# One fused block for the first two feed-forward tiles, and attention operands laid over other memory

## The chip, the cores and the metric

The kernel runs on 1 core of one Trainium2 chip. The metric is the device time of one execution in microseconds (us). Before the change it is 1364.41 us, the median of 3 runs (1362.14 to 1365.34). About the engines' names: PE is TensorE (matmuls; PEld is its weight load), DVE is VectorE, ACT is ScalarE, POOL is GpSimd, and SP is SyncE, which here only issues transfers (DMAs), in order, from its queue (SPq).

## The reference

One layer of a streaming encoder is computed for two sets of tokens with the same weights: 1024 frames of a new stream (the prompt) and 32 frames of a running one (the sample), 1056 tokens in all, model width 1024.

```python
h = x * (1 + sc1) + sh1                       # sh, sc, g: modulation, silu(c) @ w_ada + b_ada
mq, mk, mv, mo, mi, mf, fq, fk, fv, ff, gu, gv = split(h @ w_in)
hm = mlstm(mq, mk, mv, mi, mf)                # 4 heads, matrix memory
hf = fox(fq, fk, fv, ff)                      # 8 heads, softmax attention with a forget term
hg = gu * (ws @ layer_norm(gv) + bs)          # spatial gate
x = layer_norm(ALPHA * x + (1 + g1) * (concat(hm, hf, hg) @ w_o))
h = x * (1 + sc2) + sh2
y = (silu(h @ w_gate) * (h @ w_up)) @ w_down  # width 2816 = 22 tiles of 128
x = layer_norm(ALPHA * x + (1 + g2) * y)
```

The outputs are both sets' x and the caches of the three mixers.

## The kernel before, in words

**Numbers.** All products are float32 with each operand split in two float32r parts, hi and lo; `gemm` (L110) does three matmuls per 128 rows of depth: hi x hi (L116), hi x lo (L117), lo x hi (L118). A weight unit of 1024 columns is loaded as `raw`, cast to `whi` on ACT (L104) and split to `wlo` on DVE (L105), all in `weights` (L92). There are three buffers of each (`RAW = 3`, `WB = 3`).

**Tokens.** They are cut in two parts: part 0 has tokens 0 to 511, part 1 the other 544. Part 0 is worked on in two halves, 0 to 255 and 256 to 511 (`MM[0]`), or whole (`WIDE`). Part 0's attention queries are done in the first third of the kernel, and part 0 then goes through the output projection, the first normalization and the feed-forward product while part 1's attention heads (`mixers`, L1326) are worked on between its matmuls.

**The stage of the change**, in the order in which `run` (L1341) emits it:

- `wo_range` (L1041): output projection of part 0, first half, then second half. The second half is woven with `ln1` (L1079), the normalization of the first half: the two generators take turns. `ln1` makes the operand of the feed-forward product, `hh` and `hl` (shown as tm_ah and tm_al in the profile).
- `ln1` of the second half, then `fm_unit` for heads 5 to 7 (part 1's queries and keys, fm_g in the profile), whose results `evac_qk` (L358) stores to memory through the tiles qkh, qkl and qkr, and `ln1_res` (L1098) on POOL.
- Pools p1 and sm, both on the right side of the on-chip memory, are closed, and pool mx1, on the same side, is opened over them. It holds the attention's operands (k1, k2, qp, q2, v), softmax tiles and the mLSTM's tiles. A tile in it waits for the tiles that lay at its place.
- `mixers`: for each of the 8 heads `fox` (L737) loads the operands with nine transfers on SP, then for query tiles 4 to 7 does scores (L779, L780), maximum (L783), exponential (L788), division (L796), then transposes (L815), splits (L820, L821) and the product with v (L823, L828). Before head 1 stands `fox_sample` (L861), and heads 1 to 5 are woven with one mLSTM step each (L584).
- The feed-forward loop over groups of tiles: `up` (L1126) for each tile j (gate product, up product, then silu by exponential, logarithm and exponential on ACT, L1143 to L1145, two multiplications on DVE, L1146 and L1147, and the split, L1148 and L1149), then `down` (L1272) for the group. Group 0 takes tiles 0 to 3 before its `down`. After each of tiles 0 to 3 stands `ada` (L170), a modulation unit (20 to 23), which loads its weights into two of the three `raw` buffers and takes one PSUM bank of pool pg.

Tile 0 is done in halves, tiles 1 and on `WIDE` (512 columns). Pool pg has 3 PSUM banks (`NB[0]`), pool pss, for the scores, has 2.

**What sets the order.** The program text is not the order of execution. The framework simulates the program when it is built; on each engine it takes, at each simulated moment, the earliest instruction of the text that is ready. `high_priority` moves a part up in that order. `issue_after(ins)` puts what its block emits on the engine of `ins` behind `ins`, on that engine's queue alone. The resulting order of each engine is fixed in the program: on the chip, each engine takes its instructions in that order and waits when one isn't ready. So feed-forward work of later text runs in the gaps of the heads' work, and heads' instructions stand between feed-forward matmuls in PE's queue.

## Time and profile before

| | |
|---|---|
| median of 3 runs | 1364.41 us |
| the profiled execution's own time | 1365.29 us |
| its span, first to last instruction | 1363.5 us |
| mean granted TensorE clock | 0.995 |
| PE busy in 400 to 500 us of the span | 94.93 us |
| PE busy in 500 to 600 us of the span | 100.00 us |
| first matmul of feed-forward tile 0 | 444.68 us |
| first score of head 0, part 1 | 459.26 us |
| first matmul of tile 1 | 462.06 us |

The profile is one execution as the hardware recorded it. Its page gives the busy time of each engine, the span in 40 slices, the chain that ended last and the costliest groups of instructions. Further views of the same trace give busy times by window, each engine's waits with what released them, and the instructions in order of time. Names such as up_g are phase and tile: up_g is a PSUM bank of the feed-forward phase, fox_s a bank of scores, up_raw a weight buffer being loaded. Matmuls are pipelined, so what counts is the distance between their starts and not the duration of one.

### The profile page before, as it was taken

What the parts mean: (1) busy time and instruction counts of PE and PEld (TensorE: products, weight loads), DVE (VectorE), ACT (ScalarE), POOL (GpSimd) and SP (SyncE); (2) the same over time, 40 slices, a digit from 0 to 9 for tenths busy, and PEclk for the clock granted to TensorE, in tenths of its full rate; (3) what the DMA queues carried; (4) which work ended last, traced back from release to release, by engine and by line L of the source; (5) the groups of instructions that cost most, each with busy time, mean ns of one, the idle gap of its engine ahead of it and who ended that gap; (6) DMA issues with size and microseconds to landing.
All of it is one profiled execution on the core that took longest, in us unless ns stands there. A gap on an engine that the chain in (4) does not pass through costs nothing.

```text
span 1363.5 us, 25192 instructions
## 1 busy us (share of the span) xinstructions
PE 1330.9 (98%) x9434; PEld 1216.1 (89%) x9434; DVE 994.7 (73%) x2129; ACT 657.3 (48%) x1306; POOL 226.6 (17%) x263
## 2 busy tenths in 40 slices
PE   7999999999999999999999999999999999999996
PEld 4898889998999777888887888999999999999995
DVE  5545563679769667786776765678988988889777
ACT  3314454545436644545545354436664554545355
POOL 0202000053124200000000000373710000000341
PEclk9999999999999999999999999999999999999998
DMA  9765564447364765454344333574596758464321
GB/s 360 272 233 152 158 205 153 156 141 216 117 222 134 213 187 170 118 155 136 105 123 119 109 105 129 156 181 124 166 253 169 205 150 223 138 177 128 98 80 66
DMA packets 120377, 221.70 MB, mean 163 GB/s; under 512 B 18740, under 2 KB 64464, under 8 KB 120256
## 3 DMA queue, kind: packets, MB, share of 16 engines
q1 hardware_dynamic: 113024, 207.55, 48.1%
q0 software_dynamic: 6032, 11.94, 5.2%
q8 instruction: 74, 1.21, 0.4%
q10 hardware_dynamic: 1200, 0.62, 0.2%
q14 instruction: 47, 0.39, 0.1%
HBM read 188.13 MB, written 51.85 MB: 176 GB/s over the span
## 4 chain that ended last, share of the span: by engine, by line
PE 84%; DVE 6%; DMA 5%; ACT 2%; issue 1%; SPq 1%; POOL 0%; DVEq 0%; ACTq 0%
PE up_g L117 5%; PE up_g L118 5%; PE up_g L116 5%; PE dn_g L116 4%; PE dn_g L118 4%; PE dn_g L117 4%; PE tm_g L281 3%; PE tm_g L282 3%; PE tm_g L283 3%; PE sup_u L118 3%; PE sup_u L116 3%; PE sup_u L117 3%; PE fox_t L815 2%; PE sup_g L117 2%; PE sup_g L118 2%; PE sup_g L116 2%
## 5 line engine op out<-in xcount | busy, mean ns | idle before, releaser
L117 PE MATMUL up_g<-tm_al,up_whi 128*128 128x512 f32 (+1 forms) x384 | 140.3, 366 | 0.7 <-DVE tm_al L1096 0.7
L116 PE MATMUL up_g<-tm_ah,up_whi 128*128 128x512 f32 (+1 forms) x384 | 140.7, 368 | 0.1
L118 PE MATMUL up_g<-tm_ah,up_wlo 128*128 128x512 f32 (+1 forms) x384 | 139.9, 365 | 0.0
L1215 ACT CAST sup_whi<-sup_raw 128x1024 fp32r<-128x1024 f32 x54 | 56.0, 1048 | 90.6 <-PE dn_u L117 47.1
L116 PEld LDWEIGHTS up_g<-tm_ah,up_whi 128*128 128x128 f32 x384 | 72.2, 189 | 12.3 <-issue 0.8
L117 PEld LDWEIGHTS up_g<-tm_al,up_whi 128*128 128x128 f32 x384 | 72.4, 189 | 11.3 <-DVE tm_al L1096 0.9
L118 PEld LDWEIGHTS up_g<-tm_ah,up_wlo 128*128 128x128 f32 x384 | 72.4, 189 | 11.1 <-DVE up_wlo L105 0.5
L788 ACT ACTIVATE fox_p<-fox_s,fox_fmx 128x384 f32<-128x384 f32 (+2 forms) x96 | 55.2, 579 | 43.9 <-DVE fox_fmx L786 36.5
L1216 DVE TENSOR_TENSOR sup_wlo<-sup_raw,sup_whi 128x1024 fp32r<-128x1024 f32 x54 | 68.1, 1264 | 10.8 <-ACT sup_whi L1215 10.8
L105 DVE TENSOR_TENSOR up_wlo<-up_raw,up_whi 128x1024 fp32r<-128x1024 f32 x50 | 65.7, 1315 | 13.6 <-ACT up_whi L104 13.0
L1070 DVE SCALAR_TENSOR_TENSOR wo_z<-dn_g,start_mod,wo_z 128x512 f32<-128x512 f32 (+4 forms) x120 | 60.3, 521 | 20.8 <-PE dn_g L118 20.4
L104 ACT CAST up_whi<-up_raw 128x1024 fp32r<-128x1024 f32 x50 | 52.4, 1049 | 47.2 <-PE up_g L117 15.2
L116 PE MATMUL dn_g<-up_acth,dn_whi 128*128 128x512 f32 (+2 forms) x200 | 74.1, 371 | 0.0
L118 PE MATMUL dn_g<-up_acth,dn_wlo 128*128 128x512 f32 (+2 forms) x200 | 73.4, 367 | 0.0
L117 PE MATMUL dn_g<-up_actl,dn_whi 128*128 128x512 f32 (+2 forms) x200 | 72.9, 365 | 0.0
L820 ACT CAST fox_pth<-fox_t 128x512 fp32r<-128x512 f32 (+1 forms) x80 | 41.1, 545 | 59.7 <-PE fox_t L815 59.5
L104 ACT CAST dn_whi<-dn_raw 128x1024 fp32r<-128x1024 f32 (+1 forms) x44 | 42.7, 971 | 52.5 <-PE dn_u L117 10.8
L783 DVE TENSOR_REDUCE fox_fmx<-fox_s 128x1 f32<-128x384 f32 (+2 forms) x96 | 52.7, 553 | 10.7 <-PE fox_s L780 9.4
L821 DVE TENSOR_TENSOR fox_ptl<-fox_t,fox_pth 128x512 fp32r<-128x512 f32 (+1 forms) x80 | 49.5, 631 | 14.5 <-ACT fox_pth L820 14.1
L105 DVE TENSOR_TENSOR dn_wlo<-dn_raw,dn_whi 128x1024 fp32r<-128x1024 f32 (+1 forms) x44 | 49.5, 1126 | 12.7 <-ACT dn_whi L104 12.2
L281 PE MATMUL tm_g<-tm_whi,start_h1h 128*128 128x256 f32 (+1 forms) x192 | 56.0, 292 | 2.1 <-ACT tm_vhl L711 2.1
L282 PE MATMUL tm_g<-tm_wlo,start_h1h 128*128 128x256 f32 (+1 forms) x192 | 55.8, 291 | 0.0
(667 smaller groups left out, 4810.2 us busy)
## 6 DMA issues: line engine op xcount, KB each, us to landing
up_raw<-w_gu SPq DMA_DIRECT2D x50, 512.0 KB
dn_raw<-w_dn SPq DMA_DIRECT2D x28, 512.0 KB
ada_late<-w_ada SPq DMA_DIRECT2D x24, 512.0 KB
sup_raw<-w_gu SPq DMA_DIRECT2D x20, 512.0 KB
start_dp<-w_gu SPq DMA_DIRECT2D x19, 512.0 KB
start_dp<-w_gu POOLq DMA_DIRECT2D x19, 512.0 KB, 7.9
wo_raw<-w_o SPq DMA_DIRECT2D x18, 512.0 KB
sup_raw<-start_dp SPq DMA_DIRECT2D x18, 512.0 KB
```

What stands on the lines that cost most here:

```text
L104: nc.scalar.copy(hi[:, :w], raw[:, :w])
L105: (eng or nc.vector).tensor_tensor(lo[:, :w], raw[:, :w], f(hi[:, :w]), ALU.subtract)
L116: nc.tensor.matmul(ps, hi, xh(k), start=start and k == 0, stop=False)
L117: nc.tensor.matmul(ps, hi, xl(k), start=False, stop=False)
L118: nc.tensor.matmul(ps, lo, xh(k), start=False, stop=stop and k == n - 1)
L281: nc.tensor.matmul(ps[:, :ncol], xh, hi, start=k == 0, stop=False)
L282: nc.tensor.matmul(ps[:, :ncol], xh, lo, start=False, stop=False)
L783: nc.vector.tensor_reduce(mxs[:, x:x + 1], s[:, :w], AX.X, ALU.max, negate=True)
L788: nc.scalar.activation(pr[:, lo:hi], banks[x][:, :hi - lo], AF.Exp, bias=mxs[:, 0:1], accum_out=sums[:, x:x + 1])
L1070: self.lastz = self.nc.vector.scalar_tensor_tensor(z[:, m, x:y], ps[:, x - a:y - a], g[i], z[:, m, x:y], ALU.mult, ALU.add)
L1215: nc.scalar.copy(h, x)
L1216: tt(l, x, f(h), ALU.subtract)
```

## The change

Six edits:

1. A new function `up_pair` takes the place of `up` for tiles 0 and 1 and is emitted before `mixers`. In each half it does gate 0, up 0 and gate 1 (gate 1 of both halves in one PSUM bank), and the three weight units stay in their buffers for both halves. Then follows up 1 on all 512 columns.
2. The instructions that head 0 emits up to its first `yield` (loads, the scores and softmax of its first query tile) are traced with `issue_after(self.lastup.ins)`: on PE they stand behind the last matmul of the halves.
3. For head 1's mLSTM step, the part up to its first `yield` (loads and the four activations L607 to L609 and after) stands, on ACT, behind the last exponential of head 0.
4. The tiles qkh, qkl and qkr move from pool sm to a new pool sq, opened between p1 and sm; wsp (2048 bytes a partition) moves from p1 to sm.
5. The second half of `wo_range` is no longer woven with `ln1` of the first half; that follows it.
6. Modulation units 20 and 21, still emitted in the loop, are now emitted one behind the other before tile 2, and behind `up_pair` and `mixers`.

```diff
--- before.py
+++ after.py
@@ -115,7 +115,7 @@
             hi, lo = w[k][0][:, cols], w[k][1][:, cols]
             nc.tensor.matmul(ps, hi, xh(k), start=start and k == 0, stop=False)
             nc.tensor.matmul(ps, hi, xl(k), start=False, stop=False)
-            nc.tensor.matmul(ps, lo, xh(k), start=False, stop=stop and k == n - 1)
+            self.lastmm = nc.tensor.matmul(ps, lo, xh(k), start=False, stop=stop and k == n - 1)
 
 
     def constants(self):
@@ -359,9 +359,9 @@
         nc = self.nc
 
         def evac(o, n, ps):
-            hi = self.t(self.sm, [P, 272], F32R, "qkh", 2)
-            lo = self.t(self.sm, [P, 272], F32R, "qkl", 2)
-            kr = self.t(self.sm, [P, 272], F32, "qkr", 2)
+            hi = self.t(self.sq, [P, 272], F32R, "qkh", 2)
+            lo = self.t(self.sq, [P, 272], F32R, "qkl", 2)
+            kr = self.t(self.sq, [P, 272], F32, "qkr", 2)
             nc.scalar.activation(hi[:, :n], ps, AF.Copy, scale=self.qsc)
             nc.vector.scalar_tensor_tensor(lo[:, :n], ps, self.qsc, f(hi[:, :n]), ALU.mult, ALU.subtract)
             if act:
@@ -408,7 +408,7 @@
         nc.scalar.copy(k1[lo], ps[hi])
         nc.scalar.activation(q2[lo], ps[lo], AF.Copy, scale=0.125)
         for o in (0, 256):
-            kr = self.t(self.sm, [P, 272], F32, "qkr", 2)
+            kr = self.t(self.sq, [P, 272], F32, "qkr", 2)
             nc.scalar.copy(kr[hi, :256], ps[hi, o:o + 256])
             self.store(self.d["o_kT"][h, :, o:o + 256], kr[hi, :256])
         self.store(self.dqh[h, hi, :512], f(k1[hi]))
@@ -425,7 +425,7 @@
         nc = self.nc
 
         def evac(o, n, ps):
-            r = self.t(self.sm, [P, 272], F32, "qkr", 2)
+            r = self.t(self.sq, [P, 272], F32, "qkr", 2)
             nc.scalar.activation(r[:, :n], ps, AF.Copy, scale=scale)
             self.store(self.dmqk[:, i, o:o + n], r[:, :n])
         return evac
@@ -785,8 +785,8 @@
             if len(cuts) > 1:
                 nc.vector.tensor_tensor(mxs[:, 0:1], mxs[:, 0:1], mxs[:, 1:2], ALU.min)
             for x, (lo, hi) in enumerate(cuts):
-                nc.scalar.activation(pr[:, lo:hi], banks[x][:, :hi - lo], AF.Exp, bias=mxs[:, 0:1],
-                                     accum_out=sums[:, x:x + 1])
+                self.lastexp = nc.scalar.activation(pr[:, lo:hi], banks[x][:, :hi - lo], AF.Exp, bias=mxs[:, 0:1],
+                                                    accum_out=sums[:, x:x + 1])
             if len(cuts) > 1:
                 nc.vector.tensor_tensor(sums[:, 0:1], sums[:, 0:1], sums[:, 1:2], ALU.add)
             nc.vector.reciprocal(sums[:, 0:1], sums[:, 0:1])
@@ -1154,6 +1154,43 @@
 
 
 
+    def up_pair(self, act, pool):
+        self.phase = "up0"
+        nc, hh, hl, cuts = self.nc, self.hh[0], self.hl[0], MM[0]
+        for j in range(2):
+            act[j] = [self.t(pool, [P, GN[0]], F32R, x, 5) for x in ("acth", "actl")]
+        sil = [self.t(self.p2, [P, 544], F32, "sil", 2) for _ in range(2)]
+        bank = lambda: self.t(self.pg, [P, 512], F32, "g")
+
+        def product(p, w, a, b):
+            self.gemm(p, w, slice(0, P), lambda k: hh[a][:, k, :b - a], lambda k: hl[a][:, k, :b - a])
+
+        def gate(j, g, u, a, b):
+            s, (ah, al) = sil[j][:, a:b], act[j]
+            nc.scalar.activation(s, g, AF.Exp, scale=-1.0)
+            nc.scalar.activation(s, s, AF.Ln, bias=self.one)
+            nc.scalar.activation(s, s, AF.Exp, scale=-1.0)
+            nc.vector.tensor_tensor(s, g, s, ALU.mult)
+            nc.vector.tensor_tensor(s, u, s, ALU.mult)
+            nc.scalar.copy(ah[:, a:b], s)
+            self.lastact = nc.vector.tensor_tensor(al[:, a:b], s, f(ah[:, a:b]), ALU.subtract)
+
+        src = self.d["w_gu"]
+        w = self.up_weights(0) + [self.weights(src[1][:, 0:1024], KT, P)]
+        last = None
+        for a, b in cuts:
+            ps = [bank() for _ in range(2)]
+            for p, x in zip(ps, w):
+                product(p[:, :b - a], x, a, b)
+            if last is None:
+                last = bank()
+            gate(0, ps[0][:, :b - a], ps[1][:, :b - a], a, b)
+            product(last[:, a:b], w[2], a, b)
+        self.lastup = self.lastmm
+        p = bank()
+        product(p, self.weights(src[1][:, 1024:2048], KT, P), *WIDE[0])
+        gate(1, last, p, *WIDE[0])
+
     def sums(self):
 
 
@@ -1333,8 +1370,15 @@
             if h == 1:
                 self.fox_sample()
             parts = [self.fox(h, ((4, 5), (6, 7)))]
+            if h == 0:
+                with self.tc.issue_after(self.lastup.ins):
+                    next(parts[0])
             if h in MLB:
-                parts.append(slow(self.mlstm(self.nextm)))
+                part = self.mlstm(self.nextm)
+                if h == 1:
+                    with self.tc.issue_after(self.lastexp.ins):
+                        next(part)
+                parts.append(slow(part))
                 self.nextm += 1
             weave(*parts)
 
@@ -1369,13 +1413,14 @@
         self.ph = self.pool("ph")
         s1 = ExitStack()
         self.p1 = self.pool("p1", ctx=s1, side="right")
+        self.sq = self.pool("sq", 2, ctx=s1, side="right")
         self.sm = self.pool("sm", 2, ctx=s1, side="right")
         self.h1t = [self.wide_tiles(), [self.t(self.p1, [P, KT, GN[1]], F32R, x) for x in ("h1h", "h1l")]]
         self.hs = self.t(self.p1, [P, KT, 2 * NS], F32R, "hs")
         self.G = self.t(self.p1, [P, 9, 16], F32, "G")
         nc.gpsimd.memset(self.G, 0.0)
         self.rowp = self.t(self.cst, [P, 784], F32, "rowp")
-        self.wsp = self.t(self.p1, [P, 4, P], F32, "wsp")
+        self.wsp = self.t(self.sm, [P, 4, P], F32, "wsp", 1)
         self.col = self.t(self.cst, [P, 9, 4, 4], F32, "col")
         w2, w3 = d["w_in"], d["w_in_f"]
         s0 = ExitStack()
@@ -1469,7 +1514,8 @@
             kept = {}
             weave(self.wo_range(st, *MM[0][0], range(KT), kept, pw))
             del kept[3], kept[4]
-            weave(self.wo_range(st, *MM[0][1], (0, 5, 6, 7, 3, 4, 1, 2), kept, pw), self.ln1(0, st, *MM[0][0]))
+            weave(self.wo_range(st, *MM[0][1], (0, 5, 6, 7, 3, 4, 1, 2), kept, pw))
+            weave(self.ln1(0, st, *MM[0][0]))
         weave(self.ln1(0, st, *MM[0][1]))
         for h in range(PRE, 8):
             self.fm_unit(w3[2 + h], self.evac_qk(h, True), (1,))
@@ -1478,11 +1524,12 @@
         s4 = ExitStack()
         self.mx = self.pool("mx1", ctx=s4, side="right")
         self.foxbufs = (2, 1, 1, 1, 2)
-        self.mixers()
         s5 = ExitStack()
         pa = self.pool("pa0", ctx=s5)
         self.pu, self.utag = self.pg, "gg"
         act = {}
+        self.up_pair(act, pa)
+        self.mixers()
         last = len(GROUPS) - 1
         for g, (j0, nj) in enumerate(GROUPS):
             if g == WOB:
@@ -1512,7 +1559,8 @@
                 weave(fill(), norm())
                 continue
             for j in range(j0 + (g > 0), j0 + nj + (g < last)):
-                weave(self.up(0, j, act, pa, WIDE if 0 < j < GROUPS[-1][0] else MM[0]))
+                if j > 1:
+                    weave(self.up(0, j, act, pa, WIDE if j < GROUPS[-1][0] else MM[0]))
                 if j < 4:
                     self.ada(20 + j, self.wp, "raw", RAW, self.pg, "g")
             if g == WOB - 1:
```

## The prediction

> **What bounds the kernel now.** I read the page first: how much of the span TensorE (PE) is busy. Then the busy times by window, to find where it is not. Then its waits, the timeline around the feed-forward start, and the chain that ended last.
>
> ```profile
> span 1363.5 us, 25192 instructions
> PE 1330.9 (98%) x9434; PEld 1216.1 (89%) x9434; DVE 994.7 (73%) x2129; ACT 657.3 (48%) x1306; POOL 226.6 (17%) x263
> ...
> 500.00:600.00 100.00, 100.00 (x580) 82.61 (x579) 75.18 (x165) 50.57 (x111) 1.90 (x4) 0.99 0.55 159
> 450.00:462.00 12.00, 8.99 (x75) 7.53 (x74) 7.18 (x19) 6.87 (x19) 8.15 (x10) 1.00 0.84 210
> 495.00:503.00 8.00, 6.06 (x51) 4.22 (x50) 4.17 (x9) 3.26 (x9) 0.00 (x0) 0.79 0.68 212
> ```
>
> In a window row the columns are length, PE, weight loads, DVE, ACT, POOL, then granted clock, DMA share and GB/s. From 500 to 600 us PE is busy 100.00 of 100: it is the bound, and time won on it early is kept unless a later wait takes it back. The change sits where PE idles twice: 12.00 - 8.99 = 3.01 us in 450 to 462, and 8.00 - 6.06 = 1.94 us in 495 to 503, where the clock is also 0.79: 0.21 x 8 = 1.7 us of pace. Together 6.6 us, the most that can be won here.
>
> ```profile
> PE fox_s L779 <- DMA fox_k<-start_dqh: 2.2, 1, 2.2
> PE fox_t L815 <- DVE fox_p L796: 1.1, 1, 1.1
> PE fox_o L823 <- DVE fox_ptl L821: 0.9, 1, 0.9
> PE up_g L117 <- DVE tm_al L1096: 0.7, 1, 0.7
> ```
>
> These are all of PE's waits from 400 to 510 us. The first stretch is head 0's scores standing in PE's queue before their keys have landed (2.2), and the first feed-forward tile waiting for the second half of its operand (0.7). The second is head 0's softmax arriving late (1.1 and 0.9). The chain shows why it was late:
>
> ```profile
> 448.68 3.72 POOL wo_z L1105
> ...
> 457.51 7.43 DMA foxs_k<-cache_k
> ...
> 466.75 6.38 DMA up_raw<-w_gu
> 473.15 1.06 ACT up_whi L104
> 474.23 1.23 DVE up_wlo L105
> ...
> 475.49 5.34 DMA up_raw<-w_gu
> ...
> 483.19 3.67 DMA up_raw<-w_gu
> ...
> 489.21 4.36 DMA up_raw<-w_gu
> ...
> 494.67 1.23 DVE up_wlo L105
> 495.90 0.60 DVE fox_ptl L821
> ```
>
> SP issues transfers in order. Head 0's nine loads (452.11 to 457.46, next fence) and the sample's cache load stand in front of the weights of tile 2; then one weight buffer is loaded, cast, split and loaded again, four times, and the split at 494.67 stands in front of head 0's split on DVE.
>
> **The change, part by part.** *The operands' place.* The old pool sm held both early tiles and the q/k tiles of the last projections; head 0's operands lie over both.
>
> ```profile
> SPq L85 <- DMA o_kT<-fm_qkr: 1.1, 1, 1.1
> ...
> 452.11 0.47 SPq L85 DMA_DIRECT2D fox_qp<-start_dqh  x1
> ...
> 456.73 0.73 SPq L85 DMA_DIRECT2D fox_v<-start_dv  x1
> ```
>
> The loads begin at 452.11, after the store of the last projected key tile, which the first row names. By the tile sizes in the code, the new pool sq takes the q/k tiles out, and wsp fills sm, so that both key tiles, both query tiles and k2 lie over tiles finished before 400 us; v still meets sq. So the loads for the scores can go out at any time from the 430s on, and 5.3 us of SP's queue is free from 452. This alone removes the 2.2 us wait.
>
> *The pair.* Before, tile 0 ran as 96 matmuls of 256 columns, tile 1 as 48 of 512. Now 144 narrow ones (gate 0, up 0, gate 1, first half, then second half) and 24 wide ones (up 1): the same columns.
>
> ```profile
> 444.68 0.28 PE L116 MATMUL up_g<-tm_ah,up_whi 128*128 128x256 f32 x1
> ...
> 450.23 0.28 PE L118 MATMUL up_g<-tm_ah,up_wlo 128*128 128x256 f32 x1
> ...
> 462.06 0.40 PE L116 MATMUL up_g<-tm_ah,up_whi 128*128 128x512 f32 x1
> ...
> 469.76 0.39 PE L116 MATMUL up_g<-tm_ah,up_whi 128*128 128x512 f32 x1
> ```
>
> 47 steps in 5.55 us are 0.118 us for a narrow one, 33 steps in 7.70 us are 0.233 for a wide one; two narrow cost 0.236, so 24 pairs cost 0.07 more: nothing. The first half now lasts 72 x 0.118 = 8.5 us, to 453.2 instead of 450.3, and the narrow block to 444.7 + 17.0 = 461.7.
>
> ```profile
> 432.59 0.41 DVE L1096 TENSOR_TENSOR tm_al<-lna_tmp,tm_ah 128x256 fp32r<-128x256 f32 x1
> ...
> 452.15 0.42 DVE L1146 TENSOR_TENSOR up_sil<-up_g,up_sil 128x256 f32<-128x256 f32 x1 [0.19 <-ACT up_sil L1145]
> ...
> 453.37 0.41 DVE L1147 TENSOR_TENSOR up_sil<-up_g,up_sil 128x256 f32<-128x256 f32 x1
> ...
> 456.32 0.95 DVE L1096 TENSOR_TENSOR tm_al<-lna_tmp,tm_ah 128x256 fp32r<-128x256 f32 x2
> ```
>
> The second half's last k lands at 457.27; gate 0 would want it at 453.2 + 21 x 0.118 = 455.7. Up 0 and gate 1 have 48 matmuls to put in its place, so I charge 0.3 (0 to 1.6). The pair uses all three PSUM banks; the two that it needs again come free at 452.57 and 453.78, and are wanted at 453.2 and 456.0: nothing. Without that cover it is what gate 0's three activations are late by. First stretch: -3.0 + 0.3 = **-2.7**.
>
> *Three weight buffers held.* Gate 0's buffer comes free when its second half is multiplied (456 to 458); up 1's weights then need 1.06 + 1.23 us, so about 460.7, and are wanted at 461.7: nothing. If the block ended gate 0 last, 2.4 us less the four scores: up to 1.8.
>
> *The order of normalization.* ln1's first half now follows the projection's second half, instead of being woven in. Its last row was at 432.59 and is wanted at 444.68, 12 us of cover; the second half's sums can only come sooner. Nothing (-0.3 to 0).
>
> *The ties.* Head 0's first four scores now stand behind the block's last matmul on PE, so at 461.7.
>
> ```profile
> 459.26 0.56 PE L779 MATMUL fox_s<-fox_k,fox_qp 128*128 128x384 f32 x2 [2.22 <-DMA fox_k<-start_dqh]
> ...
> 466.76 0.42 ACT L607 ACTIVATE mlstm_mo<-mlstm_mo 128x256 f32<-128x256 f32 x1 [0.76 <-DMA mlstm_mo<-start_dmo]
> ...
> L788 ACT ACTIVATE fox_p<-fox_s,fox_fmx x96: 367/582/712, 139.0 to 820.9; 128x384 f32<-128x384 f32 x40, 128x512 f32<-128x512 f32 x32, 128x256 f32<-128x256 f32 x16, 128x128 f32<-128x128 f32 x8
> ...
> L116 PE MATMUL up_u<-tm_ah,up_whi x48: 276/280/483, 868.0 to 949.2; 128*128 128x256 f32 x48
> ```
>
> That is 2.4 us later than the 459.26 of the first row; if up 1's product goes first, 5.6 more. Queued behind the scores on PE is only later work of the same priority, and behind them in the data is head 0's softmax on DVE and ACT. The last softmax exponential is at 820.9 and the group-5 tile that needs the heads done begins at 868.0: 47 us of cover, so nothing. The mLSTM step's activations on ACT now wait for head 0's last exponential instead of standing at 466.76 in front of the softmax, where ACT idled 0.76; only the mLSTM output, also due by 868, waits for them. Nothing.
>
> *The weights behind the pair.* The four modulation units (ada) take two weight buffers each, and there are three. Units 20 and 21 stood between tiles 0, 1 and 2; now both come behind the pair and the heads, in front of tile 2.
>
> ```profile
> 454.83 1.07 PE L178 MATMUL ada_g<-ada_raw,start_c 128*32 128x256 f32 x16
> ...
> 475.92 0.85 SPq L85 DMA_DIRECT2D ada_raw<-w_ada  x2
> ...
> 490.90 1.07 PE L178 MATMUL ada_g<-ada_raw,start_c 128*32 128x256 f32 x16
> ```
>
> The last two rows are unit 22: loaded at 475.92, multiplied at 490.90, two of three buffers held for 15 us, which is why the chain above recycles a single one. Unit 20 ran at 454.83 in one of PE's waits, in a PSUM bank that the pair now holds. If it goes as soon as a bank is free (462), tile 2's load leaves at about 463 and its split is done 3.67 to 6.38 + 2.3 us later, 469 to 472; PE has up 1 to 467.3, four scores (0.6), and two units (2 x 1.0), so work to 469.9. If it goes behind up 1 and the scores, the load leaves at 468.9 and the weights are ready at 474.9 to 477.6, less 1.5 us of further scores that fit in: 3.5 to 6.2 us of idle. I take **+1.0**, nearer the early end, because the transfers in front of tile 2's are gone; bounds 0 and 6.2.
>
> *The second stretch.* The chain that made head 0 late began with SP's queue and the cache load; both now move ahead of 452. But PE arrives 2.7 us earlier too, and casts still share ACT and DVE with the softmax. Of 1.94 + 1.7 = 3.6 I take 60%: **-2.2** (0 to -3.6).
>
> ```profile
> 499.00:500.00 1.00, 0.72 (x4) 0.72 (x5) 1.00 (x3) 0.22 (x1) 0.00 (x0) 0.74 0.99 393
> 500.00:501.00 1.00, 1.00 (x13) 0.52 (x15) 0.15 (x1) 0.00 (x0) 0.00 (x0) 0.50 1.00 408
> ...
> 502.00:503.00 1.00, 1.00 (x5) 0.83 (x4) 0.00 (x0) 0.53 (x1) 0.00 (x0) 0.55 0.75 196
> ```
>
> These rows show the clock at half from about 499.5 to 502.5, after waits of 0.9 and 1.1 us with little between them, while the 2.22 us wait at 457 left it at 1.00. The Trainium skill, "TensorE: Matmul & The Clock Gate", Part 1, says that the clock drops to half after an idle window of about 3.4 us. By that rule neither wait would halve it, the stretch would hold 1.94 us and 60% of it would be 1.2; the trace disagrees, with 0.50 in the row of 500.
>
> **Sum.** -2.7 + 1.0 - 2.2 = -3.9 us. The profiled execution took 1365.29 us, 1.8 outside its span of 1363.5; it becomes 1361.4, with a span of 1359.6. It lies 0.9 above the median of the three runs, 1364.41, which becomes **1360.5**. With every term at its bound the sum runs from -3.0 - 0.3 - 3.6 = -6.9 to -3.0 + 1.6 + 1.8 + 6.2 = +6.6.
>
> **The rivals.**
>
> *Everything closes.* Unit 20 finds a bank early and nothing is late: -3.0 - 3.6 = -6.6, 1357.8. For it: DMA share in 450 to 462 is 0.84, and falls if 5 us of head loads move forward. Against it: only three weight buffers.
>
> *The wait moves.* The first stretch is won and tile 2's weights give the same back: -2.7 + 3.5, and half of the 2.2 won in the second stretch, -1.1: -0.3, 1364.1 (1362 to 1367). This is also how the change would fail to do what it says: the scores come on time, and PE still idles the same sum.
>
> *Slower: the weights of tile 2 stand behind units 20 and 21.* Place: PE from 469 to 477. Price: -2.7 + 6.2 of idle, the second stretch kept, and another 1.7 us of half clock as in the row of 495 to 503: +5.2, so 1369.6. It decides when tile 2's split ends later than about 473, that is, when unit 20 runs behind up 1. For it: priority by program order, and the held PSUM banks. Against it: SP's queue and the DMA engines are free by then. Without the half clock it is +3.5, 1367.9.
>
> By the same section of the Trainium skill's page, "TensorE: Matmul & The Clock Gate", idle time of that length halves the clock, so the page speaks for the dearer price; no row here has such a gap.
>
> **How the numbers follow.** Forecast 1360.5, chance 0.45, own range 1358.3 to 1362.5. All closes, 0.15. The wait moves, 0.20. Slower, 0.20. Two in ten are to be left out: I cut above 1368 and below 1357, where the whole gain would be in the pair. About 0.2% (2.7 us) is what a measurement of this kernel can tell from no change: faster means under 1361.7, slower above 1367.1. Faster: 0.40 of the forecast's 0.45 and all of 0.15, 0.55. Within: 0.05 and 0.17 of the moving wait, 0.22. Slower: 0.03 and 0.20, 0.23.
>
> **What would show it.** Right: no wait of fox_s on its key load; head 0's loads on SP before 452; PE near 12 of 12 in 450 to 462; the narrow block without a gap of over 0.5 us. Tile 2's casts on ACT before 471, with no wait on their load above 1.5 us. A clock of 1.00 from 495 to 503. Wrong: a PE gap between the last wide matmul of up 1 and the first of tile 2, with ACT waiting on up_raw; or unit 20's matmuls behind 467. A difference that arises beyond 520 us, where nothing was edited, would mean that the reordered instruction streams matter more than the two stretches, and this argument would be wrong as a whole.

## The result, and the profile after

| | before | after |
|---|---|---|
| median (us) | 1364.26 of 4 runs (1362.14 to 1365.34) | 1372.13 of 4 runs (1370.85 to 1373.05) |
| ratio, 95 % interval | | 1.0059 [1.0042, 1.0076] |
| the profiled execution, its span (us) | 1365.29, 1363.5 | 1370.85, 1369.1 |

The change makes the kernel 7.9 us slower. It was forecast 3.9 us faster, and 1372.1 lies outside the range. The two profiled executions differ by 5.6 us and not by 7.9: the one before took 1.0 us longer than its median, the one after is the fastest of its four. The section on why the prediction was wrong takes the 5.6 us apart.

The same windows of the kernel after (length, PE, weight loads, DVE, ACT, POOL, clock, DMA share, GB/s):

```profile
450.00:462.00 12.00, 9.31 (x76) 8.91 (x76) 7.19 (x18) 7.97 (x19) 7.86 (x8) 1.00 1.10 226
462.00:470.00 8.00, 5.07 (x20) 4.06 (x19) 5.60 (x13) 5.25 (x14) 0.00 (x0) 0.79 0.52 162
470.00:485.00 15.00, 12.89 (x73) 7.91 (x72) 7.93 (x24) 5.89 (x12) 0.00 (x0) 0.89 0.44 141
495.00:503.00 8.00, 8.00 (x70) 5.18 (x70) 6.96 (x15) 4.69 (x11) 0.38 (x1) 1.00 0.48 116
500.00:600.00 100.00, 99.68 (x580) 81.09 (x580) 71.44 (x156) 48.78 (x109) 2.82 (x5) 1.00 0.52 149
```

PE is still the bound from 500 us on (99.68 of 100 us). Of the two stretches that were to close, 450 to 462 idles 2.69 us where it idled 3.01, and 495 to 503 is full at full clock. In exchange there are two new ones: 2.93 us idle in 462 to 470 and 2.11 us in 470 to 485, each with a low clock. PE's longest waits from 440 to 560 us (us in total, times, longest):

```profile
PE up_g L116 <- DVE up_sil L1173: 2.9, 1, 2.9
PE up_g L116 <- DVE up_sil L1174: 1.4, 1, 1.4
PE ada_g L178 <- DMA ada_raw<-w_ada: 1.4, 1, 1.4
PE up_g L117 <- DVE tm_al L1096: 1.2, 1, 1.2
```

The wait of the scores for their keys is gone. The longest wait is now that of up 1's first matmul for a PSUM bank: L1173 is gate 0's multiplication in the new function (L1170 to L1172 are its exponential, logarithm and exponential). The chain that ended last says why it was late:

```profile
451.61 6.85 DMA fox_v<-start_dv
458.47 4.26 DMA mlstm_mb<-start_dM
462.76 0.70 DVE mlstm_mw L615
463.49 1.28 ACT mlstm_mw L618 x4
464.76 0.41 ACT up_sil L1171
465.19 0.43 ACT up_sil L1172
465.64 0.43 DVE up_sil L1173
466.12 0.72 PE up_g L116
```

L615 and L618 belong to head 1's mLSTM step and have nothing to do with up 1. They stand ahead of gate 0 on DVE and ACT, which take their instructions in order. ACT did the first activation in time, and then:

```profile
460.18 0.38 ACT L1170 ACTIVATE up_sil<-up_g 128x256 f32<-128x256 f32 x1
463.49 1.28 ACT L618 ACTIVATE mlstm_mw<-mlstm_mw,start_col 128x128 f32<-128x128 f32 x4 [2.92 <-DVE mlstm_mw L615]
464.67 0.49 ACT L1171 ACTIVATE up_sil<-up_sil,start_ones 128x256 f32<-128x256 f32 x1
```

Gate 0's logarithm, ready at 460.6, runs at 464.67, and PE idles from 463.2, the end of head 0's first scores, to 466.12. Then 8 wide matmuls run at half pace (0.43 us apart instead of 0.233).

The second new stretch is modulation unit 20, which runs behind up 1, and what follows it:

```profile
473.46 0.63 PE L178 MATMUL ada_g<-ada_raw,start_c 128*32 128x256 f32 x6
...
476.53 0.80 SPq L85 DMA_DIRECT2D up_raw<-w_gu  x2
```

Of its 2.11 us, PE waits 1.4 us for unit 21's own weights (the row of L178 among the waits) and 0.5 us for the split of tile 2's.

Of the signs that the prediction named, three came true: the scores don't wait, head 0's nine loads are issued from 446.54 to 451.61, and the clock is 1.00 from 495 to 503. The narrow block has two gaps, 1.44 and 1.25 us, PE is busy for 9.31 of 12 us in 450 to 462, and unit 20's matmuls stand behind 467. Far behind the change nothing differs: from 560 to 868 us PE is busy for all of the 308 us, at full clock, before and after.

### The profile page after: what moved, and what is told of

Read it like the earlier page. It is cut to its first block, busy times and chain, and to the rows that moved or that the text cites. A ratio compares the mean times of both kernels' runs of the same rounds, so it can differ in the third digit from the quotient of the medians.

```text
span 1369.1 us, 25240 instructions
## 1 busy us (share of the span) xinstructions
PE 1334.4 (97%) x9458; PEld 1217.0 (89%) x9458; DVE 998.2 (73%) x2129; ACT 657.4 (48%) x1306; POOL 224.9 (16%) x263
## 4 chain that ended last, share of the span: by engine, by line
PE 84%; DMA 6%; DVE 5%; ACT 3%; issue 1%; SPq 1%; ACTq 0%; DVEq 0%
PE up_g L116 5%; PE up_g L118 5%; PE up_g L117 5%; PE dn_g L116 4%; PE dn_g L118 4%; PE dn_g L117 4%; PE tm_g L281 3%; PE tm_g L282 3%; PE tm_g L283 3%; PE sup_u L118 3%; PE sup_u L116 3%; PE sup_u L117 3%; PE fox_t L815 2%; PE wo_g L117 2%; PE wo_g L116 2%; PE wo_g L118 2%
## 5 line engine op out<-in xcount | busy, mean ns | idle before, releaser
L783 DVE TENSOR_REDUCE fox_fmx<-fox_s 128x1 f32<-128x384 f32 (+2 forms) x96 | 52.6, 553 | 11.9 <-PE fox_s L780 10.8
```

The costliest lines, as they stand in the source:

```text
L783: nc.vector.tensor_reduce(mxs[:, x:x + 1], s[:, :w], AX.X, ALU.max, negate=True)
```

## The experiments

Three theories were on record. The **queue theory**: the mLSTM step in front of gate 0 on ACT and DVE, while the pair holds all three banks. The **bank theory**: modulation unit 20's last load is issued at 445.42, but it finds no bank until 473.46, so tile 2's weights, behind it in the buffers, are issued at 476.53 (466.75 before). The **weave theory**: the normalization that is no longer woven in delays the second half's operand.

All results, each with its ratio to the kernel before on the same chip. The runs were on several chips, on which the kernel before took 1363.33 to 1364.56 us, so medians of different rows can be off by about 1 us against each other. The last four columns are of one profiled execution each: PE's idle time in 440 to 560 us (120 less the PE column of that window), the number of stretches of 3.4 us at half clock in it, the loss (idle time and 1.71 us for each stretch), and the us from the first matmul of tile 0 to the first matmul of the group-5 tile that needs the heads done (up_u, at 868.0 before).

| kernel | median (us) | ratio, 95 % | idle | half | loss | to group 5 |
|---|---|---|---|---|---|---|
| before | 1364.26 | | 5.00 | 1 | 6.7 | 423.3 |
| after | 1372.13 | 1.0059 [1.0042, 1.0076] | 8.04 | 2 | 11.5 | 431.3 |
| e1_step_behind | 1364.76 | 1.0006 [0.9993, 1.0019] | 4.82 | 2 | 8.2 | 426.0 |
| e2_ada_bank | 1368.37 | 1.0041 [1.0025, 1.0056] | 7.40 | 2 | 10.8 | 427.7 |
| e3_woven | 1365.52 | 1.0014 [1.0001, 1.0027] | 5.04 | 1 | 6.8 | 425.0 |
| e4_place | 1365.27 | 1.0004 [0.9990, 1.0017] | 5.92 | 0 | 5.9 | 423.4 |
| e5_step_bank | 1366.31 | 1.0017 [1.0006, 1.0028] | 4.28 | 0 | 4.3 | 423.4 |
| e6_step_woven | 1365.28 | 1.0002 [0.9992, 1.0012] | 4.01 | 2 | 7.4 | 425.0 |
| e7_step_ada20 | 1374.96 | 1.0073 [1.0055, 1.0091] | 10.02 | 3 | 15.1 | 432.4 |
| e8_no_tie | 1374.11 | 1.0067 [1.0049, 1.0085] | 8.47 | 4 | 15.3 | 434.7 |
| e9_two_banks | 1366.73 | 1.0014 [0.9997, 1.0030] | 4.13 | 1 | 5.8 | 425.4 |
| e10_mb_first | 1370.75 | 1.0047 [1.0030, 1.0063] | 7.22 | 3 | 12.3 | 430.2 |
| e11_banks_step | 1368.61 | 1.0029 [1.0015, 1.0043] | 4.35 | 1 | 6.1 | 425.4 |
| e12_banks_step_woven | 1365.39 | 1.0003 [0.9985, 1.0022] | 5.13 | 0 | 5.1 | 423.5 |
| e13_units_later | 1371.08 | 1.0057 [1.0039, 1.0075] | 8.81 | 3 | 13.9 | 431.2 |
| e14_units_later_woven | 1368.25 | 1.0033 [1.0022, 1.0044] | 5.17 | 2 | 8.6 | 425.3 |
| e15_no_pair | 1372.86 | 1.0070 [1.0052, 1.0088] | 9.78 | 3 | 14.9 | 431.1 |

The last column sorts the kernels in two groups: up to 427.7 us the medians are 1364.3 to 1368.6, from 430.2 us on 1370.8 to 1375.0. Within a group it doesn't order them: runs of one kernel spread over 2 to 11 us, and a profile is one of them. Ahead of this stretch the executions differ too (it begins between 441.5 and 445.8 us), and behind it hardly (495.3 to 496.8 us are left).

**The queue.** e1_step_behind puts the step's second part behind gate 0 (`gates` holds its last exponential, on ACT, and its last multiplication, on DVE):

```diff
+        def behind(part):
+            with self.tc.issue_after(self.gates[0].ins), self.tc.issue_after(self.gates[1].ins):
+                next(part)
+            yield
+            yield from part
...
                         next(part)
+                    part = behind(part)
                 parts.append(slow(part))
```

> The changed kernel, with the second part of head 1's mLSTM step (its mask addition L615 on DVE and its four exponentials L618 on ACT) queued behind gate 0's last multiplication on DVE and behind gate 0's last exponential on ACT. Queue theory: gate 0's second half waited 2.92 us on ACT behind that step, which waited for a transfer, so up 1 started 2.93 us late and then ran 8 matmuls at half clock (about 1.6 us). Then the wait of up_g for up_sil L1173 (2.9 us) falls below 0.5, the clock in 465 to 470 goes from 0.66 to about 1.0, and the time falls by 4.5 us, from 1372.1 to about 1367.6. Bank theory (modulation unit 20 finds no PSUM bank until 473, so tile 2's weights leave at 476.5): the wait goes, but PE then waits as long for tile 2's weights, 1371 to 1373.

Measured 1364.76, 7.4 below the change: the queue theory's direction and more than its 4.5 (5.3 by the last column). PE's longest waits:

```profile
PE up_g L116 <- DVE up_sil L1174: 1.4, 1, 1.4
PE up_g L117 <- DVE tm_al L1096: 1.3, 1, 1.3
PE ada_g L178 <- DMA ada_raw<-w_ada: 1.2, 1, 1.2
```

The wait for L1173 is gone, up 1 starts right behind the scores, and nothing as long came in its place. e8_no_tie removes the tie that the change put on the step's first part:

```diff
-                    with self.tc.issue_after(self.lastexp.ins):
-                        next(part)
+                    next(part)
```

> The changed kernel without its third edit: head 1's mLSTM step isn't tied behind head 0's last exponential. Its activations L607 to L609 now stand on ACT in front of up 1's weight cast, and its exponentials L618 still in front of gate 0's second activation. Queue theory: the wait for up 1's bank stays at 2.9 us or grows by what the transfer of mlstm_mo is late, so 1372 to 1376. If the tie itself cost the time (by pushing work behind the softmax): 1365 or less. Bank theory: no change, 1371.5 to 1372.7.

Measured 1374.11, inside the queue theory's range, but not by its path: the wait for up 1's bank is 2.5 us, no longer than after the change, and what is added is half clock, four windows instead of two. ACT in this kernel:

```profile
462.16 0.42 ACT L607 ACTIVATE mlstm_mo<-mlstm_mo 128x256 f32<-128x256 f32 x1 [4.33 <-DMA mlstm_mo<-start_dmo]
...
464.54 1.26 ACT L618 ACTIVATE mlstm_mw<-mlstm_mw,start_col 128x128 f32<-128x128 f32 x4
465.71 0.49 ACT L1171 ACTIVATE up_sil<-up_sil,start_ones 128x256 f32<-128x256 f32 x1
```

The step is ahead of gate 0 without the tie too, and its first part, with a wait of 4.33 us, now as well. So the tie isn't the cause, it covers half of the step; whether the 2.0 us between the two medians are real the intervals don't tell. e10_mb_first moves the transfer instead of the instruction:

```diff
+        mb = t([P, 4, P], "mb", 1)
+        self.load(mb[:L, :, :L], self.dM[4 * j:4 * j + 4, :L].partition_broadcast(L))
         qk = t([P, 4, P], "mqk", 2)
...
-        mb = t([P, 4, P], "mb", 1)
-        self.load(mb[:L, :, :L], self.dM[4 * j:4 * j + 4, :L].partition_broadcast(L))
```

> The changed kernel with one transfer moved: each mLSTM step loads its row of maxima (mlstm_mb) first of its six loads instead of last, so the transfer that L615 waited 4.56 us for is issued some 4 us earlier. The banks and the ties are as in the change; the four exponentials L618 still stand in front of gate 0's activations, 1.3 us of work. Queue theory: only the wait matters, so the wait of 2.93 us for up 1's bank falls to 0 to 0.5, the half clock behind it goes, and the time falls by 4 to 7 us, to 1365 to 1368. If the place of the four exponentials in the queue matters by their own length, 1.3 us of the wait stay, 1368 to 1370.

Measured 1370.75: both expectations missed. SP's issue, and ACT:

```profile
448.69 0.47 SPq L85 DMA_DIRECT2D fox_qp<-start_dqh  x1
...
456.65 0.37 SPq L85 DMA_DIRECT2D mlstm_mb<-start_dM  x1
```

```profile
464.37 1.28 ACT L618 ACTIVATE mlstm_mw<-mlstm_mw,start_col 128x128 f32<-128x128 f32 x4 [4.63 <-DVE mlstm_mw L615]
465.56 1.03 ACT L104 CAST up_whi<-up_raw 128x1024 fp32r<-128x1024 f32 x1
```

Counted from head 0's first load, the transfer is issued 4.0 us earlier (7.96 against 11.93 us), but L615 starts only 1.3 us earlier (14.95 against 16.22): a place further ahead in SP's queue buys little here. The DMA share in 450 to 462 is 1.07; that this is the reason isn't shown. And in this build L618 stands even in front of up 1's weight cast: ACT idles 4.63 us for it with the cast behind, and PE waits 2.5 us for the cast and then 1.5 us for the bank.

**The bank.** e9_two_banks leaves the queue as it is and gives the second half's gate 0 and up 0 banks of another pool:

```diff
-            ps = [bank() for _ in range(2)]
+            ps = [bank() if a == 0 else self.t(self.pt, [P, 512], F32, "t") for _ in range(2)]
```

> The changed kernel, but gate 0 and up 0 of the second half go to the two PSUM banks of the transposes' pool; the mLSTM step's exponentials still stand on ACT in front of gate 0's second activation. If the loss is the chain queue, then bank (gate 0's late activations hold the bank that up 1 needs): up 1 takes a bank that came free before 453, so the waits for up_sil L1173 (2.93 us) and L1174 (1.44 us) go although ACT is as late as before, the half clock of 466 to 469 (1.6 us) goes, the wait for tm_al L1096 grows to at most 2.7 us, and the time is 1364 to 1366, as in e1_step_behind (1364.8). If late activations cost the time in another way (through head 0's softmax behind them on ACT): 1370 to 1372. Bank theory for unit 20 (a bank free from 452): tile 2's weights leave before 470, and another 2 us go, 1362 to 1364.

Measured 1366.73, 5.4 below the change (5.9 by the last column). ACT, then PE's waits:

```profile
465.53 1.28 ACT L618 ACTIVATE mlstm_mw<-mlstm_mw,start_col 128x128 f32<-128x128 f32 x4 [1.68 <-DVE mlstm_mw L615]
466.72 0.49 ACT L1171 ACTIVATE up_sil<-up_sil,start_ones 128x256 f32<-128x256 f32 x1
```

```profile
PE up_t L117 <- DVE tm_al L1096: 2.9, 1, 2.9
PE up_g L116 <- ACT up_whi L104: 1.1, 1, 1.1
```

L618 still holds ACT, but up 1 begins at 465.91, before gate 0's logarithm at 466.72: the late ACT no longer holds up 1 once it has another bank. The wait for L1174 has turned into a longer one for the operand. Tile 2's weights were issued at 473.88, later than the bank theory said. e2_ada_bank gives units 20 and 21 a bank instead:

```diff
         self.up_pair(act, pa)
+        for u in (20, 21):
+            self.ada(u, self.wp, "raw", RAW, self.pt, "t")
         self.mixers()
...
-                if j < 4:
+                if 1 < j < 4:
```

> The changed kernel, with modulation units 20 and 21 traced directly behind the pair and given a PSUM bank of the transposes' pool (pt) in place of one of the three that the pair holds; the order of the weight buffers stays. Bank theory: unit 20's weights were there at 446 to 450 and only the bank was missing until 473.5; now it runs in PE's waits at 450 to 454, tile 2's weights are issued at about 465 instead of 476.5, PE's idle time of 475 to 485 (1.6 + 0.5 us) and its half clock there (1.65 us) go, and the time falls by about 3.7 us to 1368.4. Queue theory: the wait of 2.93 us at 463 stays as it is, and what is won behind it is at most the 2.1 us of idle, 1370 or more.

Measured 1368.37, the bank theory's number, by luck: tile 2's weights do leave early (467.61), but PE's longest wait is now 5.3 us instead of 2.93, for unit 21's copy L181, which stands behind the same step on ACT:

```profile
470.12 1.28 ACT L618 ACTIVATE mlstm_mw<-mlstm_mw,start_col 128x128 f32<-128x128 f32 x4 [4.72 <-DVE mlstm_mw L615]
...
471.79 0.35 ACT L181 COPY ada_adas<-ada_t 128x256 f32<-128x256 f32 x1
```

e5_step_bank is the edits of e1_step_behind and e2_ada_bank together.

> Both edits of the first two runs together: the mLSTM step behind gate 0 (e1_step_behind, 1364.8) and units 20 and 21 in a bank of the transposes' pool (e2_ada_bank, 1368.4, where PE stood 5.33 us behind unit 21's copy L181, which stood on ACT behind the mLSTM step). If queue and bank are separate causes, they add: 1364.8 - 3.8 = 1361.0, with tile 2's weights issued before 470 and no wait above 2 us in 450 to 485. If the bank only brings unit 21 in front of up 1 in PE's and ACT's queues, where its own transfer (1.5 us late in e2_ada_bank) is waited for: 1363 to 1365, no better than e1_step_behind.

Measured 1366.31: no better than e1_step_behind, and above both expectations. By its profile it loses nothing in the stage (423.4 us to group 5, the same as before); 1.3 us more than before come behind that, and the rest of the 2 us isn't placed. e11_banks_step is e9_two_banks and e1_step_behind together.

> e9_two_banks and e1_step_behind together. If both edits cut the same chain at two places (the queue in the one, the bank in the other), together they give what the better one gives: within 1 us of it, 1363 to 1365. If they are separate losses of 7.4 us and a further 2 to 4: 1361.

Measured 1368.61, above both expectations. In the profile the two don't add: 425.4 us to group 5, as e9_two_banks alone, with its waits within 0.1 us. That fits two cuts of one chain. The profiled execution took 1364.32, the fastest of its ten; it began tile 0 at 441.53, 2.4 us before that of e9_two_banks. Why its median is above that kernel's stays open.

**The weave.** e3_woven undoes edit 5, and e6_step_woven does so on top of e1_step_behind:

```diff
-            weave(self.wo_range(st, *MM[0][1], (0, 5, 6, 7, 3, 4, 1, 2), kept, pw))
-            weave(self.ln1(0, st, *MM[0][0]))
+            weave(self.wo_range(st, *MM[0][1], (0, 5, 6, 7, 3, 4, 1, 2), kept, pw), self.ln1(0, st, *MM[0][0]))
```

> The changed kernel, with the second half of the output projection again woven with the first half's normalization. Weave theory: the waits at the start of the second half of the pair (1.44 us for up_sil L1174 and 1.25 us for tm_al L1096) come from the normalization's late place in DVE's queue, so they fall to before's 0.7 in all and the time falls by about 2 us to 1370. Queue and bank theories: the later waits and the half clock stay, 1371.5 to 1372.7, the place of the first matmul of the pair moves back from 442.2 to about 444.7.

> The mLSTM step behind gate 0 (e1_step_behind, 1364.8) and the projection woven with the normalization again (e3_woven, 1365.5). In e3_woven the mLSTM step's exponentials had come to stand behind gate 0's activations without being tied there. If that, and not the weave itself, made its gain of 6.6 us, the weave is worth nothing more once the step is tied: 1364.8 to 1365.5. Weave theory: the waits for up_sil L1174 and tm_al L1096 (1.4 and 1.3 us in e1_step_behind) fall as well, 1362 to 1363.

Measured 1365.52 and 1365.28. The first alone, 6.6 below the change, looks like proof of the weave theory. But its build also moved the step behind gate 0 (here already behind gate 1):

```profile
465.92 0.63 ACT L1172 ACTIVATE up_sil<-up_sil 128x512 f32<-128x512 f32 x1
466.45 1.27 ACT L618 ACTIVATE mlstm_mw<-mlstm_mw,start_col 128x128 f32<-128x128 f32 x4
```

With the step tied, the weave is worth nothing that can be told from noise (1364.76 against 1365.28). The two waits that it was to shorten, 1.4 and 1.3 us, have become one of 2.0 us, for the multiplication of gate 0's first half (up_sil L1173). e12_banks_step_woven adds it to e11_banks_step.

> e11_banks_step with the projection woven with the normalization again. Weave theory: the operand's second half is then the last wait of the pair (1.25 to 2.7 us for tm_al L1096) and the weave takes a part of it away, 1 to 2 us below e11_banks_step. If the weave only changes the order far from the wait, as e6_step_woven against e1_step_behind (+0.5): within 1 us of e11_banks_step.

Measured 1365.39, equal to the kernel before within its interval and 3.2 below e11_banks_step, more than expected, with intervals that just overlap. In its profile the operand's wait is 0.8 us in place of 2.9, so the weave does shorten that one wait; a later head's queries now cost 2.4 us.

**The weights.** e13_units_later and e14_units_later_woven move units 20 and 21 behind tile 2, in e11_banks_step and e12_banks_step_woven; e7_step_ada20 takes e1_step_behind, gives unit 20 another bank as e2_ada_bank does, and puts 21 and 22 behind tile 2, 23 behind tile 3:

```diff
-                if j < 4:
-                    self.ada(20 + j, self.wp, "raw", RAW, self.pg, "g")
+                for u in {2: (20, 21), 3: (22, 23)}.get(j, ()):
+                    self.ada(u, self.wp, "raw", RAW, self.pg, "g")
```

> e1_step_behind with unit 20 alone traced behind the pair in a bank of the transposes' pool, and unit 21 moved behind tile 2, together with unit 22. Bank theory: tile 2's loads then wait for neither unit, leave before 465, PE's idle time of 2.2 us in 470 to 490 and its half clock there (1.7 us) go: 1364.8 - 3.5 = 1361.3. If the three units in a row only move the same wait to tile 3: 1364 to 1366, with a gap of PE between 485 and 500.

> e11_banks_step (two more banks and the mLSTM step behind gate 0; in its profile PE still waits 2.9 us for the operand's second half and 1.2 us for tile 2's weight cast) with modulation units 20 and 21 moved behind tile 2 and units 22 and 23 behind tile 3. Weights theory (units 20 and 21 hold two of the three weight buffers in front of tile 2): tile 2's loads leave before head 0's, at about 450, PE's wait of 1.2 us and the 0.1 to 0.5 us beside it go, and the time is 1.5 us below e11_banks_step. Transfer theory (the DMA engines are full from 450 to 460, share 1.06 to 1.11, so a load moved forward only delays the next one): head 0's keys or gate 0's neighbours on ACT wait instead, and the time is the same as e11_banks_step or up to 3 us above.

> The same move in e12_banks_step_woven (1365.4; its profile waits 1.6 us for tile 2's cast, 0.8 us for the operand and 2.4 us for a later head's queries). Weights theory: 1363 to 1364, which would be below the kernel before. Transfer theory: 1365 to 1368, with a new wait of the scores or of ACT for a transfer between 455 and 475.

Measured 1374.96 (e7_step_ada20), 1371.08 (e13_units_later) and 1368.25 (e14_units_later_woven): each slower than the kernel that it was made from, by 10.2, 2.5 and 2.9 us, the last two with intervals that overlap or touch. In e7_step_ada20 the queue theory shows once more, with another culprit: tile 2's own weight cast came to stand before gate 0's second exponential, its transfer was late, and up 1 waited 7.46 us:

```profile
471.62 1.04 ACT L104 CAST up_whi<-up_raw 128x1024 fp32r<-128x1024 f32 x1 [3.94 <-DMA up_raw<-w_gu]
```

In e13_units_later PE waits 3.9 us for weight casts of later tiles and 1.2 for those of the down product. There the weights' wait moves on to the next tile; it doesn't go.

**Single edits.** e4_place is the kernel before with edit 4 alone. e15_no_pair is the changed kernel with edits 3 to 5 alone:

```diff
-        self.up_pair(act, pa)
...
-                if j > 1:
-                    weave(self.up(0, j, act, pa, WIDE if j < GROUPS[-1][0] else MM[0]))
+                weave(self.up(0, j, act, pa, WIDE if 0 < j < GROUPS[-1][0] else MM[0]))
```

> The kernel before, with only the memory edit: the q/k tiles in a pool of their own and wsp in sm, so that head 0's operands lie over tiles done early; no pair, no ties, no new order. If the operands' place alone takes away the 2.22 us wait of the scores for their keys and nothing comes in its stead: 1362.0. If head 0's loads were late because of SP's queue and not of their place, or the wait is only moved to the softmax: 1364.3, within 0.5. If the reordering that it brings costs as much as the pair does: over 1366.

> The changed kernel without the pair and without the tie of head 0's scores to it: the memory edit, the unwoven normalization and the tie of head 1's mLSTM step stay, tiles 0 and 1 are done as in the kernel before. Here the step's exponentials stand on ACT in front of up 1's weight cast and of gate 0's second half. If the pair's hold on all three banks is what makes a late ACT cost time: the same late ACT instruction costs at most the 1.0 to 1.5 us by which up 1's cast is late, 1363 to 1366. If the tie or the unwoven order lose the time by themselves: 1370 or more.

e4_place: 1365.27, the same as before. Head 0's loads start at 449.97 instead of 452.11, the scores still wait 2.2 us for their keys:

```profile
PE fox_s L779 <- DMA fox_k<-start_dqh: 1.5, 1, 1.5
...
PE fox_s L780 <- DMA fox_k<-start_dql: 0.7, 1, 0.7
```

e15_no_pair: 1372.86, a miss. PE's waits:

```profile
PE up_g L116 <- ACT tm_ah L1095: 3.5, 1, 3.5
PE fox_s L779 <- DMA foxs_k<-start_dsf: 3.5, 1, 3.5
```

Without the pair, tile 0's first half is shorter, and PE waits for the operand's second half and for transfers in front of the scores. This suggests that in the unwoven order the pair covers waits. The kernel is 8 us above e1_step_behind (1364.76, the pair and the step tied), but the two differ in more than the pair, so that isn't shown.

No kernel here is faster than the kernel before; the intervals of e1_step_behind, e4_place, e6_step_woven, e9_two_banks and e12_banks_step_woven hold 1, and the others are slower.

## Why the prediction was wrong

- **The operands' place: half right.** The wait of the scores went (462.44, behind the block, no wait). That "this alone removes the 2.2 us wait" was wrong: in e4_place the loads began 2.1 us earlier and the wait stayed at 2.2. Nor did the loads go out from the 430s on: the first is at 446.54.
- **The pair's pace: right; its operand: mis-sized.** 72 matmuls took 8.4 us. The block's end, 462.33 for 461.7, agrees by luck: it began 2.5 us earlier (442.17) and waited 2.69 us inside. For the operand 0.3 was charged (0 to 1.6); the 2.69 us were waited for L1174 (a bank of the second half, 1.44) and for the operand, L1096 (1.25), and with other banks it was 2.9 for the operand alone. On DVE, seven rows of the second half's normalization and a memset came first:

```profile
449.74 2.43 DVE L1088 TENSOR_TENSOR wo_z<-wo_z,wo_qs 128x256 f32<-128x256 f32 x7
...
452.77 0.91 DVE L879 MEMSET foxs_k<- 2x1024 f32 x1 [0.27 <-issue]
453.71 1.71 DVE L1096 TENSOR_TENSOR tm_al<-lna_tmp,tm_ah 128x256 fp32r<-128x256 f32 x4
```

- **The failed step:** "The pair uses all three PSUM banks; the two that it needs again come free at 452.57 and 453.78, and are wanted at 453.2 and 456.0: nothing. Without that cover it is what gate 0's three activations are late by." It counted the banks of the second half (at nothing, where 1.44 us was waited) and left out the next user, up 1, whose bank waits for gate 0's second half, behind which nothing lies but four scores of 0.6 us. The price that it names, how late the activations are, was paid: 2.93 us and 1.71 of half clock. Taking either end away (e1_step_behind, e9_two_banks) gave back 7.4 and 5.4 us of the 7.9, more than these 4.6; the rest of what they gave isn't placed.
- **The ties, the step that goes with it:** "only the mLSTM output, also due by 868, waits for them. Nothing." The tie holds L607 to L609. L615 and L618 behind the first `yield` were free to go ahead of gate 0, and I didn't ask who stands behind them.
- **The weights behind the pair: place right, size too small.** Charged 1.0 (0 to 6.2). Unit 20 ran behind up 1, tile 2's loads left at 476.53, and 470 to 485 lost 2.1 us of idle time and 1.7 of half clock: 3.8. But most of the idle time, 1.4 us, was for unit 21's own weights, which the sum had no term for, and only 0.5 for tile 2's. That is the place and much of the price of the slower rival; the time was above its 1369.6, since the bank came on top.
- **The second stretch: better than forecast.** -2.2 charged; 495 to 503 is full at full clock, -3.6 by idle time and clock.

Together, in the profiles: -0.3 + 2.9 + 1.7 + 2.1 + 1.7 - 3.6 + 0.3 (idle in 503 to 550) = +4.8. This stage is 8.0 us longer after the change: from 442.17 to up_u's first matmul at 873.4, where it was from 444.68 to 868.0. So 3.2 us aren't placed: there PE counts as busy, at full clock, and is slower at the same work. The spans differ by 5.6 because the profiled execution before lost 2.5 us ahead of the stage:

```profile
339.05:342.46 3.41, 3.41 (x18) 3.41 (x17) 2.33 (x9) 1.29 (x5) 0.00 (x0) 0.50 0.63 159
...
L116 PE MATMUL up_u<-tm_ah,up_whi x48: 277/281/484, 873.4 to 954.7; 128*128 128x256 f32 x48
```

The first row, before, is a window at half clock (1.7 us), and 100 to 200 us idles 1.62 us before and 0.62 after. That isn't the change's doing: e1_step_behind, whose one edit lies behind this point, begins the pair at 444.28.

## What to carry to other kernels

When a block takes every bank of a pool, look beyond it: the next user waits for the whole evacuation chain, and that chain stands in order behind whatever the builder put on ACT and DVE, a wait for an unrelated transfer included. A tie on one part of a step leaves its later parts free, so list the step's instructions on each engine. And when one edit rebuilds the order of all engines, check that the suspected instruction didn't move too before crediting the edit (e3_woven). Measure the stage between two instructions that both kernels have, and not by the span: here the spans differ by 5.6 us and the stage by 8.0.

## What the runs showed of the hardware

The half clock comes in pieces of 3.41 us, each 1.71 us of pace; all the episodes from 100 to 1300 us in these profiles are one, two or three of them. Windows of 3.41 us, laid so that one ends where the clock drops, in the kernel before:

```profile
455.10:458.52 3.42, 1.94 (x24) 1.23 (x16) 2.17 (x5) 1.39 (x5) 3.05 (x4) 1.00 0.91 243
458.52:461.93 3.41, 2.67 (x21) 2.67 (x22) 0.33 (x3) 0.32 (x1) 0.00 (x0) 1.00 1.11 222
...
496.06:499.48 3.42, 1.87 (x22) 1.37 (x23) 2.44 (x7) 2.60 (x7) 0.00 (x0) 1.00 0.68 165
499.48:502.89 3.41, 3.41 (x27) 2.59 (x27) 0.67 (x2) 0.42 (x1) 0.00 (x0) 0.50 0.87 316
```

and after:

```profile
449.16:452.58 3.42, 1.98 (x18) 1.78 (x16) 3.34 (x10) 3.03 (x8) 2.36 (x2) 1.00 1.03 273
452.58:455.99 3.41, 2.16 (x16) 1.96 (x17) 3.19 (x7) 2.49 (x7) 3.02 (x5) 1.00 1.11 199
462.82:466.23 3.41, 0.48 (x4) 0.28 (x3) 2.35 (x4) 2.68 (x8) 0.00 (x0) 1.00 0.55 164
466.23:469.65 3.42, 3.42 (x9) 2.66 (x10) 3.02 (x10) 2.58 (x7) 0.00 (x0) 0.50 0.41 135
476.47:479.88 3.41, 1.81 (x17) 0.66 (x12) 2.25 (x10) 1.51 (x5) 0.00 (x0) 1.00 0.89 276
479.88:483.30 3.42, 3.42 (x19) 2.51 (x11) 1.50 (x6) 2.07 (x4) 0.00 (x0) 0.50 0.83 255
```

In each kernel one grid fits the drops: 339.05 and 499.48 before are 47 windows apart, 466.23 and 479.88 after are four. Windows with 1.55, 2.93 and 1.60 us of idle time are followed by one at half clock; those with 1.48, 1.44 and 1.25 are not. By this reading the 2.2 us gap before left the clock alone because it lay across two windows (1.48 and 0.74). The 2.7 us of waits at 451 to 454 did so too, but in e1_step_behind the same waits lay mostly in one window (1.86) and halved the next. So a gap costs its length, and up to 1.7 us more if it falls badly. Over all 17 profiles, from 100 to 1300 us, each of the 18 windows at full clock with 1.74 us of idle time or more was followed by one at half clock, and 5 of the 11 with 1.48 to 1.70. Idle time alone doesn't decide it: in e1_step_behind, e6_step_woven and e15_no_pair windows with 1.0, 0.9 and 1.0 us of it also led to a drop. Those of the first two were full of scores, transposes and narrow matmuls.

The Trainium skill, "TensorE: Matmul & The Clock Gate", Part 1, says that the clock is set by a free-running window of 3413 ns and drops after an idle one. The trace agrees with the window's length and with a grid that runs on from one drop to the next; it disagrees that the window must be idle, since PE was busy for 1.87 of 3.42 us in the one before the drop at 499.48.
